# Token tiles 4 to 7 loaded a second time with channels on the partitions, normed in PSUM, their token rows rebuilt later on GpSimd

## The chip, the cores and the metric

The kernel runs on one core of a Trainium2 chip. The core has a matrix engine (PE), a vector engine (DVE), a scalar engine (ACT), GpSimd (POOL) and a queue engine (SP) from which nearly all DMAs are issued. The metric is the device time of one execution in microseconds, the median of several; lower is better. The kernel before takes 662.84 us (three runs, 662.69 to 662.87).

## The reference

One encoder layer on 1024 tokens of 1024 channels, in float32:

```
h    = layer_norm(x, emb_ln_g, emb_ln_b)             # the embedding norm
proj = h @ w_in     # q, k, v, z_attn, u, z_lru (512 columns each), g_attn, g_lru (1024 each)
attn = neighbourhood_attention(q, k, v, rpb)          # window 8 x 16 on a 16 x 64 grid, 8 heads
u    = centred_depthwise_conv(u, conv_w, conv_b)
hid  = rg_lru(u, forward) + rg_lru(u, reverse)        # decay rate: C * softplus(-lru_lambda)
m    = sigmoid(g_attn + b0) * ((attn * silu(z_attn)) @ w_ba)
     + sigmoid(g_lru + b1) * ((hid * silu(z_lru)) @ w_bb)
out  = layer_norm(alpha * h + m @ w_out, ln_g, ln_b)
```

The change touches the first line, the order of the first projections behind it, and the small polynomial for softplus(-lru_lambda).

## The kernel before, in words

**Numbers.** Every float32 operand of PE is split in two parts of PE's reduced float32 type, `_h` (a cast) and `_l` (the rest, a subtraction), and a product is three matmuls: high by high, low by high, high by low (`mm3`, L133). So each operand costs one cast (ACT or POOL) and one subtraction (DVE or POOL) before PE can use it.

**Tokens.** Eight tiles of 128 tokens. Tile i arrives token-major (`load_x`: 128 tokens on the partitions, 1024 channels along the row, 512 KB). The norm's mean and variance come from DVE (`ln_stats`, L223 to L225), the root from ACT (L229), 1/root refined on DVE (L237 to L239). Tiles 0, 1 and 3 are scaled on DVE with the gains in PSUM (L244, L247). Tiles 2 and 4 to 7 are scaled on ACT (L254) and get gain and offset on POOL (L260, four passes of 128x512). The finished tile is stored to DRAM (`keep`, `h_d`) for the residual at the end of the kernel; the store frees one of five buffers (tag `x`) for a later `load_x`. Then PE turns the tile in eight 128x128 transposes (`turn`, L271) into two PSUM banks, `tp{i}_0` and `tp{i}_1`, channels on the partitions; ACT casts these to `B..[0]` (`turn_hi`, L280), DVE makes `B..[1]` (`turn_lo`, L127).

**First products.** With the turned tiles PE computes v for each tile in 24 matmuls (`v_part`: kinds `h`, `w`, `a`, 8 each, L327; `a` uses the low parts) and a first part of q (`q_part`, four quarters of 24 matmuls of 512 columns each; the first quarter is done in two halves of 256 columns). The first two quarters need tiles 0 to 3, the last two need 4 to 7.

**Strassen's sums.** The other projections run as 17 pairs, each with seven products of 12 matmuls (`product`; one product is one *slot* of the schedule). They need sums of the turned tokens, T1, T2, T3 (from `t_full`, tiles 4 to 7, L300 to L304) and T4 (`t_last`, L308, L309), each split into high and low (`t_hi` on ACT, L313; `t_lo` on POOL). In pair 0 slot 0 and 1 use B11 and B21; T2, T1, T3 come in slots 2 to 4 and T4 in slot 6. The weights of pair p+1 are summed (`s_sum`, L385, DVE), cast (`s_hi`, L390) and split (`s_lo`) while pair p runs; a low part is made five slots ahead of its product.

**What sets the order.** All five engines run in the order in which the program text issues (`manual_schedule`), with semaphores between them. There is no planner; an instruction that waits holds back all behind it on its engine, SP's DMA issues too. From slot 0 on, work is hung into slots by hand (`at(slot, pos, f)`). PSUM has eight banks: `ps0` (0 to 3) for v and q, the others for `tp`; from slot 0 six banks go round for the products.

**Start.** PE begins with 18, 4 and 6 small bf16 matmuls on zeros (`warm_up`, L203, `WARM`), between them transposes that spread the norm's gains (`gps`, L212).

Of the kernel before, what the change touches and what calls it, by code (L numbers as in the profile page):

```python
# [45 lines left out]

SM_CW, SM_CB, SM_GB, SM_LAM, SM_BM, SM_N = 0, 16, 20, 36, 44, 60
HALVES = ((slice(0, 64), slice(64, P)), (slice(64, P), slice(0, 64)))
# [18 lines left out]
@with_exitstack  # L67
def encoder_kernel(ctx, tc, x, gb1, gb, w_qk, w_v, w_s, w_ba, w_bb, w_gate, smalls, bias, w_out, out):
    nc = tc.nc
# [42 lines left out]
    V.memset(eps_z, EPS * TWICE * TWICE)  # L112
    A.activation(warm, eps_t, AF.Sqrt)
    sm = cst.tile([P, SM_N], F32, name="sm")

# [10 lines left out]
    def lo_of(eng, lo, full, hi):  # L126
        eng.tensor_tensor(lo, full, hi.bitcast(F32), ALU.subtract)  # L127
# [103 lines left out]
    def ln_sums(i):  # L231
        ln_stats(i)
        ln_root(i)
# [28 lines left out]
    def keep(i):  # L262
        SP.dma_start(h_d[i], xs[i][:])

    tps = {}

# [23 lines left out]
    def f(t, i):  # L290
        return t[:, :, ti(i)].bitcast(F32)

    def t_full(i):

        tag = ("a22", "a21", "a12", "a22")[i - 4]
        tt[i, 3] = wsp.tile([P, 4, P], F32, tag=tag, bufs=2 if tag == "a22" else 1, name=f"t3_{i}")[:]
# [3 lines left out]
        A.copy(t3, tp4(i, 0))  # L300
        V.tensor_tensor(t1, tp4(i, 0), f(B11[0], i), ALU.subtract)
        V.tensor_tensor(t1, t1, f(B11[1], i), ALU.subtract)
        V.tensor_tensor(t2, tp4(i, 1), t1, ALU.subtract)
        V.tensor_tensor(t3, tp4(i, 1), t3, ALU.subtract)  # L304

    def t_last(i):
        t4 = tt[i, 4] = tt[i, 2]
        V.tensor_tensor(t4, f(B21[0], i), t4, ALU.subtract)  # L308
        V.tensor_tensor(t4, t4, f(B21[1], i), ALU.add)  # L309
# [58 lines left out]
    def s_load(p, *names):  # L368
        for z, o in enumerate(names if p < N_PAIR else ()):
            if p:  # L370
                t = wsp.tile([P, 4, P], F32, tag=o, bufs=2 if o == "a22" else 1, name=f"{o}_{p}f")[:]
            else:
                if z == 0:
                    place = dict(pool=ln, tag="x", bufs=5) if o == "a21" else dict(pool=wpl, tag="ws", bufs=1)
                    both = place.pop("pool").tile([P, 2, 4, P], F32, name=f"{o}_{p}f", **place)
# [11 lines left out]
    def s_hi(p, o):  # L387
        if p < N_PAIR:
            s_w[p, o] = pair(wsp, [P, 4, P], f"w{o}_{p}", tag="w" + o)
            (G.tensor_copy if p and o in HI_POOL else A.copy)(s_w[p, o][0][:], s_a[p, o])  # L390

    def s_lo(p, o):
        if p < N_PAIR:
            hi, lo = s_w[p, o]
            lo_of(G if p and o in LO_POOL else V, lo[:], s_a[p, o], hi[:])

# [109 lines left out]

    def tile_in(i):
        for kk in BOTH:
            turned_in(i, kk)

    def tile_lo(i):
        for kk in BOTH:
            turn_lo(i, kk)

    def ln_next(i):
        ln_sums(i)
        ln_scale(i)
# [37 lines left out]
    v_store(3)
    keep(6)
    q_part(0, 0, slice(256, HALF))
    tile_in(5)
    q_hi(0, 0)
    t_hi(4, 2, 1, 3)  # L560
    t_lo(4, 2, 1, 3)
    tile_lo(5)
    q_lo(0, 0)
    q_store(0, 0)
    keep(7)
    t_full(5)
    q_part(1, 0)
    q_hi(1, 0)
    q_lo(1, 0)
    q_store(1, 0)  # L570
    t_hi(5, 2, 1, 3)
    t_lo(5, 2, 1, 3)
    for kind in "hwa":
        v_part(4, kind, KS)
    tile_in(6)
    v_hi(4)
    tile_lo(6)
    v_lo(4)
    v_store(4)
    t_full(6)  # L580
    t_hi(6, 2, 1, 3)
    t_lo(6, 2, 1, 3)
    for kind in "hwa":
        v_part(5, kind, KS)
    s_load(0, "a11", "a12")
    tile_in(7)
    v_hi(5)
    tile_lo(7)
    v_lo(5)
    v_store(5)  # L590
    t_full(7)
    t_hi(7, 2, 1, 3)
    t_lo(7, 2, 1, 3)
    s_load(0, "a21", "a22")
    s_load(1, "a21")
    for kind in "hwa":
        v_part(6, kind, KS)
    v_hi(6)
    v_lo(6)
    v_store(6)  # L600
    s_load(1, "a12")
    s_sum(0, "s1", "s2", "s3", "s4")
    for kind in "hwa":
        v_part(7, kind, KS)
    v_hi(7)
    v_lo(7)
    v_store(7)
    s_load(1, "a11")
    for o in OPS[:3]:
        s_hi(0, o)  # L610
        s_lo(0, o)
    q_part(0, 1)
    for o in OPS[3:5]:
        s_hi(0, o)
        s_lo(0, o)
    q_hi(0, 1)
    q_lo(0, 1)
    q_store(0, 1)
    s_load(1, "a22")
    q_part(1, 1)  # L620
    for o in OPS[5:]:
        s_hi(0, o)
        s_lo(0, o)
    t_last(4)
    q_hi(1, 1)
    t_hi(4, 4)
    t_last(5)
    q_lo(1, 1)
    q_store(1, 1)
    for i in (5, 6, 7):  # L630
        if i > 5:
            t_last(i)
        t_hi(i, 4)
    for i in (7, 4, 5, 6):
        t_lo(i, 4)
    for pl in (ln, wpl, hb12, pst, ps0):
# [6 lines left out]
    lru = pool("lru", "right")  # L643
    sp = lru.tile([P, 8], F32, name="sp")
    nsp = lru.tile([P, 8], F32, name="nsp")
    t0, t1, t2 = (lru.tile([P, 8], F32, name=f"sp{c}") for c in range(3))
    lam = sm[:, SM_LAM:SM_LAM + 8]

    def decay_rates():
        V.tensor_scalar(smh[:], sm[:, SM_BM:SM_BM + 16], 0.5, None, ALU.mult)  # L650
        V.tensor_scalar(t0[:], lam, -1.0, None, ALU.mult)
        V.tensor_tensor(t0[:], lam, t0[:], ALU.min)
        A.activation(t0[:], t0[:], AF.Exp)
        yield
        V.tensor_scalar(t1[:], t0[:], 2.0, None, ALU.add)
        V.reciprocal(t1[:], t1[:])
        V.tensor_tensor(t0[:], t0[:], t1[:], ALU.mult)
        V.tensor_tensor(t1[:], t0[:], t0[:], ALU.mult)
        V.tensor_scalar(t2[:], t1[:], 1.0 / 21.0, 1.0 / 19.0, ALU.mult, ALU.add)
        yield  # L660
        for n in (17, 15, 13, 11, 9, 7, 5, 3, 1):
            V.tensor_tensor(t2[:], t2[:], t1[:], ALU.mult)
            V.tensor_scalar(t2[:], t2[:], 1.0 / n, None, ALU.add)
            if n in (13, 7, 1):
                yield
        V.tensor_tensor(t2[:], t2[:], t0[:], ALU.mult)
        V.tensor_scalar(t0[:], lam, -1.0, 0.0, ALU.mult, ALU.max)
        V.scalar_tensor_tensor(t0[:], t2[:], 2.0, t0[:], ALU.mult, ALU.add)
        V.tensor_scalar(sp[:], t0[:], C_LRU, None, ALU.mult)
        V.tensor_scalar(nsp[:], t0[:], -C_LRU, None, ALU.mult)  # L670
        yield
# [122 lines left out]
    def gate_stage(t, d, slot):  # L794
# [38 lines left out]
        def tables():  # L833
            A.activation(warm[:], eps_t[:], AF.Sigmoid)

# [111 lines left out]
    def gates_b(j):  # L947
# [3 lines left out]
             lambda: take_u(2), gates_b(0), lambda: take_zg(zb_d, 2, "zb"), gates_a(2), gates_b(1),  # L951
             lambda: take_k(0), gates_a(3), lambda: take_k(2), lambda: take_zg(za_d, 2, "za"), gates_b(2), gates_b(3)]
    rates = decay_rates()
    for slot in range(8, 14):
        at(slot, 1, lambda: next(rates))
# [807 lines left out]
```

## Time and profile before

| | |
|---|---|
| runs | 662.84 us median (662.69 to 662.87) |
| profiled execution, its own time | 663.5 us |
| its span, first to last instruction | 661.7 us |
| granted TensorE clock | 0.996 |
| busy: PE, DVE, ACT, POOL | 649.5, 521.6, 389.0, 396.7 us |
| slot 0 of pair 0 (first `a` matmul, timeline) | 82.78 us |

A timeline row gives the start, the duration, engine and line, the operation with output and inputs, a count, and in brackets the idle time before it with what ended it. Matmul durations overlap, since PE pipelines: the distance between two starts is what a matmul costs. The span is 1.8 us shorter than the execution's own time, and that execution was 0.66 us longer than the median.

### The profile page before, as it was taken

To read this page: it belongs to the slowest core of one execution; us is meant where nothing else is said; L and a number is where in the kernel's file an instruction comes from. 1 tells how busy PE (TensorE), PEld (TensorE's weight loads), DVE (VectorE), ACT (ScalarE), POOL (GpSimd) and SP (SyncE) were. 2 spreads that over 40 slices of the span, in tenths; PEclk is the share of its full clock that TensorE was granted. 3 is DMA by queue.
4 is the path that set the end of the run, shared out by engine and by line. 5 is a ranking of instruction groups with operands and counts; after the bars stand their busy time and mean duration, and the time that the engine had idled before them with its cause. 6 is when DMAs were issued, how large, how long until landed. Compare 5 with 4: busy or idle time off the path is not lost.

```text
span 661.7 us, 9464 instructions
## 1 busy us (share of the span) xinstructions
PE 649.5 (98%) x3119; PEld 543.5 (82%) x3119; DVE 521.6 (79%) x860; ACT 389.0 (59%) x686; POOL 396.7 (60%) x311
## 2 busy tenths in 40 slices
PE   8999999999999999999999999999999999999994
PEld 7888888888888887888788888888898888888883
DVE  7978867786899599879987696277877876994776
ACT  5564433356786677777666834277777744573242
POOL 6799263434676476658556455013552549989857
PEclk9999999999999999999999999999999999999998
DMA  8747607033334133532361548898977298333023
GB/s 324 271 140 250 195 33 257 15 111 128 125 113 135 57 112 99 188 111 81 132 220 59 192 163 281 306 342 272 362 264 240 68 306 294 113 113 127 24 104 128
DMA packets 52482, 113.42 MB, mean 171 GB/s; under 512 B 5505, under 2 KB 9937, under 8 KB 50897
## 3 DMA queue, kind: packets, MB, share of 16 engines
q1 hardware_dynamic: 51968, 112.28, 49.0%
q8 instruction: 25, 0.41, 0.2%
q10 hardware_dynamic: 464, 0.53, 0.2%
q14 instruction: 25, 0.20, 0.1%
HBM read 77.11 MB, written 35.68 MB: 170 GB/s over the span
## 4 chain that ended last, share of the span: by engine, by line
PE 86%; DVE 7%; POOL 2%; issue 1%; ACT 1%; DMA 1%; POOLq 0%; DVEq 0%; ACTq 0%
PE a L133 32%; PE s L133 12%; PE mb L133 12%; PE x L133 6%; PE w L133 5%; PE v L327 4%; PE s L1107 3%; PE acc L1155 3%; PE pt L1129 3%; PE q L133 2%; PE g L805 2%; POOL x L260 1%; DVE ws_l L127 1%; DVE uc L763 1%; PE tp L271 1%
## 5 line engine op out<-in xcount | busy, mean ns | idle before, releaser
L133 PE MATMUL a<-ht_h,ws_h 128*128 128x512 f32 x136 | 53.1, 391 | 0.0
L133 PE MATMUL a<-ht_l,ws_h 128*128 128x512 f32 x136 | 52.9, 389 | 0.0
L133 PE MATMUL a<-ht_h,ws_l 128*128 128x512 f32 x136 | 52.9, 389 | 0.0
L133 PE MATMUL a<-b_l,wa_h 128*128 128x512 f32 x136 | 52.9, 389 | 0.0
L133 PE MATMUL a<-b_h,wa_h 128*128 128x512 f32 x136 | 52.9, 389 | 0.0
L133 PE MATMUL a<-b_h,wa_l 128*128 128x512 f32 x136 | 52.9, 389 | 0.0
L1117 DVE CUSTOM_DVE_ANT_0 sc<-s,bias 128x384 f32<-128x384 f32 (+1 forms) x64 | 33.5, 523 | 20.3 <-PE s L1107 11.4
L1136 ACT CAST pt_h<-pt 128x384 fp32r<-128x384 f32 x64 | 29.0, 453 | 23.8 <-PE pt L1129 19.3
L1122 ACT ACTIVATE p<-sc,summ 128x384 f32<-128x384 f32 (+1 forms) x64 | 37.9, 592 | 5.4 <-DVE summ L1117 5.0
L133 PE MATMUL mb<-ya,wb_h 128*128 128x512 f32 x128 | 39.7, 390 | 0.1
L913 POOL CAST wb_h<-wb 128x512 fp32r<-128x512 f32 x9 | 7.0, 781 | 47.2 <-DMA wb<-in_w_bb_dram 47.2
L127 DVE TENSOR_TENSOR pt_l<-pt,pt_h 128x384 fp32r<-128x384 f32 x64 | 33.3, 520 | 1.9 <-ACT pt_h L1136 1.6
L127 POOL TENSOR_TENSOR ht_l<-t,ht_h 128x512 fp32r<-128x512 f32 x16 | 21.9, 1406 | 18.2 <-ACT ht_h L313 18.2
L1521 POOL TENSOR_TENSOR z<-z,gb 128x512 f32<-128x512 f32 (+2 forms) x23 | 27.7, 1218 | 8.5 <-ACT z L1516 7.5
L327 PE MATMUL v<-wv,b_h 128*128 128x512 f32 x128 | 32.4, 395 | 0.4 <-ACT b_h L426 0.4
L1107 PE MATMUL s<-ks,qs 128*128 128x384 f32 (+1 forms) x128 | 31.7, 329 | 0.0
L133 PEld LDWEIGHTS a<-ht_h,ws_h 128*128 128x128 f32 x136 | 25.5, 188 | 5.9 <-issue 0.5
L1129 PEld LDWEIGHTS pt<-ident,p 128*128 128x128 f32 x176 | 23.1, 140 | 8.3
L133 PEld LDWEIGHTS a<-ht_l,ws_h 128*128 128x128 f32 x136 | 25.5, 188 | 5.3
L133 PEld LDWEIGHTS a<-b_h,wa_l 128*128 128x128 f32 x136 | 25.5, 188 | 5.3
L133 PEld LDWEIGHTS a<-b_h,wa_h 128*128 128x128 f32 x136 | 25.5, 188 | 5.3
L133 PEld LDWEIGHTS a<-b_l,wa_h 128*128 128x128 f32 x136 | 25.5, 188 | 5.3
(542 smaller groups left out, 2258.9 us busy)
## 6 DMA issues: line engine op xcount, KB each, us to landing
ks<-k_d SPq DMA_DIRECT2D x8, 1024.0 KB, 7.6
h_d<-x SPq DMA_DIRECT2D x8, 512.0 KB, 2.9
v_d<-vs SPq DMA_DIRECT2D x8, 512.0 KB, 3.2
q_d<-q SPq DMA_DIRECT2D x8, 512.0 KB, 3.2
ga_d<-ga SPq DMA_DIRECT2D x16, 256.0 KB, 2.1
gb_d<-gb SPq DMA_DIRECT2D x16, 256.0 KB, 2.4
k_d<-k SPq DMA_DIRECT2D x8, 512.0 KB, 5.1
qs<-q_d SPq DMA_DIRECT2D x8, 512.0 KB, 5.2
```

What stands on the lines that cost most here:

```text
L127: eng.tensor_tensor(lo, full, hi.bitcast(F32), ALU.subtract)
L133: PE.matmul(o, a, b, start=first and i == 0, stop=last and i == len(prods) - 1, skip_group_check=not (first and last))
L327: PE.matmul(vos[i][:], a, wv[kind == "w"][k][:], start=vn[i] == 0, stop=vn[i] == 23)
L805: PE.matmul(o[:, n, :], w[:, 2 * d + b, :], us[b][:, n * HALF:(n + 1) * HALF], start=z == 0, stop=z == 1)
L913: G.tensor_copy(hi[:], st[:])
L1107: PE.matmul(o[:, :P * len(near(t))], q[:, t * P:(t + 1) * P], k[:, z, keys], start=z == 0, stop=z == 1)
L1117: V.tensor_tensor_reduce(s[:, :w], o[:, :w], heads[h][2][:, b0:b0 + w], -1.0, 3.0e38, ALU.add, ALU.min, accum_out=sums[h][0][:, t:t + 1])
L1122: A.activation(probs[h % 2][t][:], scs.pop((h, t))[:, :w], AF.Exp, bias=sums[h][0][:, t:t + 1], scale=-1.0, accum_out=sums[h][1][:, t:t + 1])
L1129: PE.transpose(tp[:, n * P:(n + 1) * P], probs[h % 2][t][:, z * P:(z + 1) * P], ident[:])
L1136: A.copy(pt[0][:, span(b)], tps[h, b][:, :P * len(near(b))])
L1155: PE.matmul(acc[n][:, lo - n * HALF:hi - n * HALF], vvs[h // 2][:, b, h % 2, :], pt[:, a:a + hi - lo], start=b in (1, 6) and z == 0, stop= ...
L1521: G.tensor_tensor(z, z, gbs[c, n][:, part], (ALU.mult, ALU.add)[c])
```

## The change

Tiles 4 to 7 are loaded twice: token-major as before, now only for mean and variance, and channel-major (`xt`, a copy that the host lays out, 128 channels on the partitions, `[P, 8, 128]`, 512 KB). PE no longer turns them. It spreads the 128 means and the 128 values of 1/root over the partitions (`spread`, two transposes of a broadcast column into one bank `bcp`). DVE subtracts the mean (`centred`, two passes of 128x512, one operand in PSUM), POOL multiplies by 1/root (two passes), and ACT applies gain and offset, which are now one number per partition, in eight passes of 128x128 that write the banks `tp{i}_0` and `tp{i}_1` (`affine`). Casting and splitting go on as before. The gains stand in `smalls` (16 more columns).

The token-major rows that the residual needs are made later: in slots 1 to 15 the four tiles are loaded a third time, scaled on ACT with the kept mean and 1/root, get gain and offset on POOL (16 passes), and are stored to `h_d`.

Other parts: the six matmuls of the third `warm_up` are left out; v of tiles 2 and 3 is cut in pieces between the spreads, and v of tiles 4 and 5 come together; `t_hi` of tiles 4 and 5 goes from ACT to POOL; T4 (`t_last`) is formed in PSUM (`pst4`, four banks), and its low parts go from POOL to DVE, with one cast of it; two of pair 0's low weights go from DVE to POOL; the casts of pairs 1 and 2 go from POOL to ACT; the softplus polynomial goes from DVE in slots 8 to 13 to POOL in slots 12 to 20.

```
-WARM = 18, 4, 6
+WARM = 18, 4, 0
+TOKENS_AT = ((1, 3, (4, 4, 5, 5)), (2, 5, (6, 6, 7, 7)), (3, 7, (8, 8, 9, 9)), (9, 11, (12, 12, 13, 13)))
+RATES_AT = (12, 13, 14, 15, 16, 17, 20)
+FIRST_POOL = ("a22", "s4")
+FIRST_ACT = (1, 2)
...
+    def sts_rest(i):
+        ln_rstd(i)
+        st, mv, sd, ve = sts[i]
+        V.tensor_scalar(kept[:, 2 * i - 8:2 * i - 7], mv[:, 0:1], -1.0, sd, ALU.mult, ALU.mult)
+        V.tensor_copy(kept[:, 2 * i - 7:2 * i - 6], sd)
+
+    def spread(i):
+
+        bcp[i] = pst.tile([P, HALF], F32, tag="bank", name=f"bcp{i}")
+        for z, col in enumerate((sts[i][1][:, 0:1], sts[i][2])):
+            PE.transpose(bcp[i][:, z * P:(z + 1) * P], col.to_broadcast([P, P]), ident[:])
+
+    def spread_copy(i):
+        bcs[i] = wsp.tile([P, 1, P], F32, tag=f"s{i - 3}", name=f"bc{i}")
+        A.copy(bcs[i][:, 0], bcp[i][:, P:2 * P])
+
+    def centred(i):
+
+        for kk in range(2):
+            t = xts[i][:, 4 * kk:4 * kk + 4, :]
+            V.tensor_tensor(t, t, bcp[i][:, :P].unsqueeze(1).to_broadcast([P, 4, P]), ALU.subtract)
+            G.tensor_tensor(t, t, bcs[i][:].to_broadcast([P, 4, P]), ALU.mult)
+
+    def affine(i, *kks):
+        for kk in kks or BOTH:
+            tps[i, kk] = pst.tile([P, HALF], F32, tag="bank", name=f"tp{i}_{kk}")
+            for k4 in range(4):
+                k = 4 * kk + k4
+                g, b = (sm[:, SM_LN + 8 * z + k:SM_LN + 8 * z + k + 1] for z in range(2))
+                A.activation(tps[i, kk][:, k4 * P:(k4 + 1) * P], xts[i][:, k, :], AF.Identity, bias=b, scale=g)
+            turn_hi(i, kk)
...
     def t_hi(i, *cs):
         for c in cs:
-            A.copy(Ts[c][0][:, :, ti(i)], tt[i, c])
+            (V.tensor_copy if (i, c) == (7, 4) else G.tensor_copy if i < 6 and c < 4 else A.copy)(Ts[c][0][:, :, ti(i)], tt[i, c])
...
     def t_lo(i, *cs):
         for c in cs:
-            lo_of(G, Ts[c][1][:, :, ti(i)], tt[i, c], Ts[c][0][:, :, ti(i)])
+            lo_of(G if c < 4 else V, Ts[c][1][:, :, ti(i)], tt[i, c], Ts[c][0][:, :, ti(i)])
...
     load_x(4)
     SP.dma_start(sm[:], smalls)
+    load_xt(4)
...
-    ln_next(5)
-    for kind in "hwa":
-        v_part(2, kind, KS)
-    keep(4)
-    ln_next(6)
...
+    v_part(2, "h", KS)
+    v_part(2, "w", KS)
+    spread(4)
+    spread_copy(4)
+    centred(4)
+    qk_prep(1)
+    stats_t(5)
+    v_part(2, "a", KS)
+    v_part(3, "h", KS)
+    v_part(3, "w", K0)
+    spread(5)
+    spread_copy(5)
+    stats_t(6)
+    centred(5)
+    v_hi(2)
+    v_part(3, "w", K1)
+    v_part(3, "a", K0)
+    spread(6)
...
+    def tokens_scaled(i):
+        n = 2 * i - 8
+        A.activation(hw[i][:], hw[i][:], AF.Identity, bias=kept[:, n:n + 1], scale=kept[:, n + 1:n + 2])
+
+    def tokens_gained(i, z, c):
+        t = hw[i][:, halves[c]]
+        G.tensor_tensor(t, t, ln_row[z][:, halves[c]], (ALU.mult, ALU.add)[z])
...
-    for slot in range(8, 14):
+    for slot in RATES_AT:
         at(slot, 1, lambda: next(rates))
```

Three places where the order on an engine differs. The first is PE at the end of the high parts of v of one tile; `x_175` is tile 4's token buffer, `v_559` is v of tile 3 before, `v_488` v of tile 2 in the change. Before:

```order
L327 MATMUL v_559<-wv_140,b_h 128x512
L327 MATMUL v_559<-wv_141,b_h 128x512
L271 MATMUL tp_0_579<-ident,x_175 128x128 x4
L271 MATMUL tp_1_585<-ident,x_175 128x128 x4
L327 MATMUL v_559<-wv_126,b_l 128x512
```

In the change (line numbers are those of the new text):

```order
L384 MATMUL v_488<-wv_146,b_h 128x512
L384 MATMUL v_488<-wv_147,b_h 128x512
L294 MATMUL bcp_505<-ident,ln4m 128x128
L294 MATMUL bcp_505<-ident,ln4e 128x128
L384 MATMUL v_488<-wv_132,b_l 128x512
```

Eight transposes of the tile have become two of its statistics, one tile of v earlier; the same holds for tiles 5, 6 and 7. The second place is DVE between the low part of v of tile 1 and the end of tile 6's statistics. Before:

```order
L127 TENSOR_TENSOR vs_426<-v_328,vs_426 128x8x64
L223 BN_STATS ln5t<-x_256 128x6 x2
L224 BN_AGGR ln5m<-ln5t 128x2
L225 TENSOR_SCALAR ln5e<-ln5m 128x1
L237 RECIPROCAL ln5e<-ln5e 128x1
L238 TENSOR_SCALAR ln5e<-ln5e 128x1
L239 TENSOR_SCALAR ln5e<-ln5e 128x1
L253 TENSOR_SCALAR ln5e<-ln5m,ln5e 128x1
L223 BN_STATS ln6t<-x_313 128x6 x2
```

In the change:

```order
L133 TENSOR_TENSOR vs_428<-v_330,vs_428 128x8x64
L304 TENSOR_TENSOR xt_184<-xt_184,bcp_505 128x512 x2
L229 BN_STATS ln5t<-x_258 128x6 x2
L230 BN_AGGR ln5m<-ln5t 128x2
L231 TENSOR_SCALAR ln5e<-ln5m 128x1
L243 RECIPROCAL ln5e<-ln5e 128x1
L244 TENSOR_SCALAR ln5e<-ln5e 128x1
L245 TENSOR_SCALAR ln5e<-ln5e 128x1
L287 TENSOR_SCALAR kept<-ln5m,ln5e 128x1
L288 COPY kept<-ln5e 128x1
L229 BN_STATS ln6t<-x_315 128x6 x2
```

Tile 4's two subtractions stand ahead of tile 5's statistics, and each tile has one small copy more. The third place is ACT behind the casts of the early tiles, in the change; `xt_184` is tile 4's channel-major copy:

```order
L298 COPY bc_508<-bcp_505 128x128
L176 CAST wqk_h<-wqk_s 128x1024
L235 ACTIVATE ln5e<-ln5m,few 128x1
L298 COPY bc_555<-bcp_552 128x128
L235 ACTIVATE ln6e<-ln6m,few 128x1
L391 CAST vs_574<-v_488 128x8x64
L298 COPY bc_587<-bcp_584 128x128
L313 ACTIVATE tp_0_589<-xt_184,sm 128x128 x4
L339 CAST b_h<-tp_0_589 128x4x128
```

Where one pass of 128x1024 (L254) and two casts stood for a tile, there are now a copy, eight passes of 128x128 and the two casts, and tile 4's first pass stands behind tile 6's spread.

More of the change, by code (lines that the diff above doesn't have):

```diff
@@ L113, in encoder_kernel @@
     A.activation(warm, eps_t, AF.Sqrt)
+    kept = cst.tile([P, 8], F32, name="kept")
+    sp, nsp, t0, t1, t2 = (cst.tile([P, 8], F32, name=f"sp{c}") for c in range(5))
     sm = cst.tile([P, SM_N], F32, name="sm")
@@ L600, in encoder_kernel @@
     v_store(6)
+    t_hi(7, 2, 1, 3)
+    t_lo(7, 2, 1, 3)
     s_load(1, "a12")
@@ L612, in encoder_kernel @@
     q_part(0, 1)
-    for o in OPS[3:5]:
+    for o in ("s1", "s3", "a22", "s4"):
         s_hi(0, o)
         s_lo(0, o)
+    t_places(4)
+    T1, T2, T3, T4 = (Ts[c] for c in (1, 2, 3, 4))
+    pst.release()
+    pst = tc.alloc_tile_pool(name="pst4", bufs=1, space=bass.MemoryType.PSUM, reuse_waits="tile")
+    for i in (7, 6, 5, 4):
+        tt[i, 4] = pst.tile([P, HALF], F32, name=f"t4_{i}")[:].rearrange("p (k t) -> p k t", k=4)
     q_hi(0, 1)
```

205 lines of the change are left out of this document (117 added, 88 removed).

## The prediction

> **What bounds the kernel now.** I read the page first: busy shares, then the chain that ended last.
>
> ```profile
> PE 649.5 (98%) x3119; PEld 543.5 (82%) x3119; DVE 521.6 (79%) x860; ACT 389.0 (59%) x686; POOL 396.7 (60%) x311
> PE 86%; DVE 7%; POOL 2%; issue 1%; ACT 1%; DMA 1%; POOLq 0%; DVEq 0%; ACTq 0%
> ```
>
> PE is busy for 98% of the span. A share is a mean, so next the busy times by stretch:
>
> ```profile
> 0.00:15.00 15.00, 13.04 (x79) 11.40 (x80) 10.90 (x27) 7.75 (x17) 8.45 (x13) 1.00 0.86 317
> ...
> 83.00:285.00 202.00, 202.00 (x888) 165.86 (x887) 169.06 (x216) 123.26 (x159) 113.67 (x86) 1.00 0.34 114
> 285.00:330.00 45.00, 44.64 (x196) 36.36 (x195) 41.33 (x37) 33.21 (x43) 31.56 (x19) 1.00 0.32 112
> 425.00:540.00 115.00, 114.77 (x690) 100.73 (x689) 87.80 (x238) 79.06 (x220) 44.18 (x41) 1.00 0.77 268
> 540.00:661.70 121.70, 112.43 (x508) 93.40 (x506) 90.03 (x162) 56.16 (x116) 103.72 (x82) 0.98 0.39 136
> ```
>
> The columns are the stretch, its length, and PE, its weight loads, DVE, ACT, POOL, then granted clock, DMA share and GB/s. PE loses 2.0 us in the first 15, 0.4 and 0.2 from 285 on, and 9.3 at the end, where the last norm runs. From 83 us on the change touches nothing that PE does, and PE has no gap worth winning there. So the time follows the moment at which slot 0 starts (82.78 us before), as long as DVE, ACT, POOL and the loads keep up behind it. The sum is therefore PE's own sequence up to slot 0, and its waits.
>
> **The change part by part.** *Start.* Six small matmuls go.
>
> ```profile
> 7.42 0.62 PE L203 MATMUL clock<-zero 128*128 128x128 bf16 x6
> 7.88 0.61 PE L271 MATMUL tp<-ident,x 128*128 128x128 f32 x4
> 9.20 0.69 DVE L127 TENSOR_TENSOR b_l<-tp,b_h 128x512 fp32r<-128x512 f32 x1 [0.28 <-ACT b_h L426]
> 14.33 0.63 PE L271 MATMUL tp<-ident,x 128*128 128x128 f32 x4 [0.30 <-DVE x L247]
> ```
>
> They cost PE 0.46 us from start to start. Behind them the path runs over ACT's cast to DVE, which waited 0.28 us for it, and DVE then runs without a gap to the norm for which PE waits at 14.33. DVE can come forward only by those 0.28, so I take 0.28 (bounds 0 and 0.46).
>
> *Transposes taken away.* Tiles 4 to 7 are turned in four groups of eight; one of them is split by a wait.
>
> ```profile
> 35.84 1.03 PE L271 MATMUL tp<-ident,x 128*128 128x128 f32 x8
> 36.63 2.07 PE L327 MATMUL v<-wv,b_l 128*128 128x512 f32 x8
> 41.42 0.60 PE L271 MATMUL tp<-ident,x 128*128 128x128 f32 x4
> 42.38 0.66 PE L271 MATMUL tp<-ident,x 128*128 128x128 f32 x4 [0.37 <-POOL x L260]
> 42.80 0.47 PE L133 MATMUL q<-b_h,wqk_h 128*128 128x512 f32 x1
> ...
> 60.14 1.03 PE L271 MATMUL tp<-ident,x 128*128 128x128 f32 x8
> 60.93 0.48 PE L327 MATMUL v<-wv,b_h 128*128 128x512 f32 x1
> ```
>
> The first and the last group here cost 0.79 us, as does one between them; the one at 41.42 costs 1.38 with its wait for POOL: 3.75 us.
>
> *Transposes added.* Four spreads of two, at 0.79 / 8 = 0.10 us each: 0.8 us. A broadcast column as the weights stood in the trace only at the start, at half the speed:
>
> ```profile
> L212 PEld LDWEIGHTS gps<-ident,gb_col x16: 226/226/226, 3.9 to 7.0; 128*128 128x128 f32 x16
> L271 PEld LDWEIGHTS tp<-ident,x x64: 137/140/143, 7.8 to 60.8; 128*128 128x128 f32 x64
> ```
>
> If that were the price of the broadcast, eight would cost 1.7 us. All 64 others ran at 140 ns, so I hold it for the slow clock of the first microseconds and take 0.8 (bounds 0.8 and 1.7). PE's own sequence is thus 0.28 + 3.75 - 0.8 = 3.2 us shorter.
>
> *New waits.* A spread needs the tile's 1/root from DVE. With everything 0.28 us earlier PE reaches the 16 transposes of tiles 2 and 3 at 24.72 and the sixteen matmuls behind them at 26.38 (these rows before, and DVE's in the same stretch):
>
> ```profile
> 25.00 1.91 PE L271 MATMUL tp<-ident,x 128*128 128x128 f32 x16
> 26.66 3.90 PE L327 MATMUL v<-wv,b_h 128*128 128x512 f32 x16
> 30.40 1.98 PE L327 MATMUL v<-wv,b_l 128*128 128x512 f32 x8
> 32.21 3.79 PE L327 MATMUL v<-wv,b_h 128*128 128x512 f32 x16
> 30.40 0.68 DVE L127 TENSOR_TENSOR vs<-v,vs 128x512 fp32r<-128x512 f32 x1
> 31.00 1.27 DVE L223 BATCH_NORM_STATS2 ln5t<-x 128x6 f32<-128x512 f32 x2
> 33.38 0.21 DVE L239 TENSOR_SCALAR ln5e<-ln5e 128x1 f32<-128x1 f32 x1
> 33.76 0.68 DVE L223 BATCH_NORM_STATS2 ln6t<-x 128x6 f32<-128x512 f32 x1
> L303 DVE TENSOR_TENSOR t<-tp,t 128x512 f32<-128x512 f32 x4 | 2.8, 692 | 0.1
> L302 DVE TENSOR_TENSOR t<-t,b_l 128x512 f32<-128x512 f32 x4 | 4.8, 1197 | 0.1
> ```
>
> Sixteen matmuls take 3.74 us, eight 1.81, one 0.227. PE: spread 4 at 30.1, spread 5 at 30.4 + 20 x 0.227 = 34.9, spread 6 at 35.2 + 1.8 = 37.0. DVE: its 31.00 becomes 30.8 (0.28 earlier, one small copy of about 0.1 later). Two subtractions come first; they are nearest to L303, which also has one operand in PSUM and starts its successor 0.6 us later; L302, with both in SBUF and POOL busy, is the other bound (1.2). So tile 5's statistics start at 32.0, and its 1/root stands 33.59 - 31.00 = 2.6 us later: 34.6, in time for 34.9. Tile 6's start 2.9 us after tile 5's (2.76 before, plus the copy), 34.9, and its 1/root is there at 37.5, with the semaphore 37.6. Spread 6 therefore waits about 0.4 us (one of its two transposes needs the mean alone). With L302's price for the subtractions both spreads are late by 1.2 more; with tile 6's x late it grows one for one. I take 0.4 (bounds 0 and 1.6). Spread 7 comes some 9 us later, behind q, and its bank is free once DVE has read `tp4_0`, which I put a good microsecond ahead of it.
>
> *What lies beside other work.* ACT gets eight passes of 128x128 for a tile in place of one of 1.25 us:
>
> ```profile
> L1516 ACT ACTIVATE w<-z,ve,sd x4: 442/762/765, 620.9 to 654.9; 128x512 f32<-128x512 f32 x3, 128x128 f32<-128x128 f32 x1
> L254 ACT ACTIVATE x<-x,ln5e 128x1024 f32<-128x1024 f32 x1 | 1.2, 1247 | 1.0 <-DVE ln5e L253 1.0
> 45.00:83.00 38.00, 38.00 (x177) 31.64 (x176) 31.75 (x45) 18.99 (x37) 24.23 (x18) 1.00 0.57 194
> ```
>
> The 128x128 form that writes PSUM took 0.44 us. Each waits for the one before it, so some 0.47 x 8 = 3.8 us a tile, 10 us more for four tiles against 1.25 x 4; ACT had 19 us free in the 38 of the last row. From spread 6 at 37.9 on, tile 4 is cast by 44, tile 5 by 50, tile 6 by 56, tile 7 by 62, and PE asks for them at about 47, 53, 58 and 64: the cover is 2 to 3 us, and a tile that is later than that is a wait of PE. On DVE, T4's low parts (four of 0.6 us and a cast) come on top of its last stretch before the slots, but slot 1 needs only tile 4's part of T4 read out of its bank, slot 3 tile 5's, slot 6 the rest. POOL's 16 token passes and 26 small ones in slots 4 to 20 stand before low weights that are due five slots of 2.7 us later. The extra loads (2 MB of `xt`, 2 MB of x, 1 MB of gains) fall into stretches with the DMA share at 0.3 to 0.6, except the first 512 KB, which stand ahead of a store that frees tile 5's buffer:
>
> ```profile
> SPq L188 <- DMA h_d<-x: 12.8, 2, 8.6
> 24.30 0.33 SPq L188 DMA_DIRECT2D x<-in_x_dram  x1
> x<-in_x_dram SPq DMA_DIRECT2D x6, 512.0 KB, 4.3
> ```
>
> SP waits up to 8.6 us for such a store, and tile 6's load comes behind tile 5's. At the 317 GB/s of the first stretch 512 KB are 1.6 us, so tile 6's load goes from 24.30 to 25.9 and lands 4.3 us later, at 30.2; it is read at 34.9. All these I set to 0.
>
> *Sum.* 3.2 - 0.4 = 2.8 us; I take 2.7, since a wait I have not seen is likelier than one less. The profiled execution's 663.5 becomes 660.8 (span 659.0), and the median, 0.66 below that execution, **660.2 us**.
>
> **The rivals.** *One: the new feed is late.* DVE and ACT are the bound in place of PE: subtractions at L302's price make spreads 5 and 6 wait 1.6 us in all, and a tile that ACT finishes 1 us after PE asks for it takes the rest: 3.2 - 2.6 = 0.6 us gained, 662.2. For it speaks that DVE must deliver within tenths; against it that L303's form never took more than 0.7 with POOL busy.
>
> *Two: slower, DVE starved by POOL in slots 4 to 13.* DVE's operations with two SBUF inputs get long when POOL works:
>
> ```profile
> L127 DVE TENSOR_TENSOR wa_l<-a_11f,wa_h 128x512 fp32r<-128x512 f32 x1 | 2.9, 2885 | 0.0
> L127 DVE TENSOR_TENSOR ws_l<-s_11f,ws_h 128x512 fp32r<-128x512 f32 x4 | 5.9, 1478 | 0.0
> L662 DVE TENSOR_TENSOR sp<-sp,sp 128x8 f32<-128x8 f32 x8 | 1.3, 165 | 0.2
> 93.90:118.60 24.70, 24.70 (x109) 20.12 (x109) 20.11 (x51) 6.82 (x12) 10.50 (x12) 1.00 0.53 182
> ```
>
> About 13 such operations fall into those ten slots (27 us). At 2.9 us each in place of 0.7 they add 29 us to DVE's roughly 17 (20.11 of 24.70, less some 26 small operations of the polynomial at 0.17, scaled to 27), 19 more than the slots last. Low weights have five slots, 13.6 us, of cover, so PE would wait 5.4 us: 660.2 + 5.4 = 665.6, slower. It decides from about 2.7 us for each (where the excess reaches 13.6 us plus the 2.7 gained). Against it: in the trace 2.9 is the extreme, 1.5 a high mean. [...]
>
> *Three: the clock comes late.* If the six matmuls are what raises the clock, PE runs at half speed for one more stretch like that of the sixteen L212 (3.4 us): 1.7 us lost, 0.3 of it in the wait at 14.33: 661.6. Against it, the weight loads were slow up to 7.0 and fast from 7.8, with only transposes in the 3.4 us before. [...]
>
> *Four: the change doesn't do what it says*, the token passes being late for the end: the rows are read after 570 us and stored near 125, so I give it nothing.
>
> **How the numbers follow.** Forecast 0.66, its own range 659.2 (nothing waits, and the later 0.6 us of PE's gaps shrink too) to 661.2; rival one 0.17, two 0.09, three 0.06, the rest unknown. The range goes to 662.2, with rival one inside. A measurement of this kernel tells 0.2%, 1.3 us, from no change: faster means below 661.5. That holds for nearly all of the forecast (0.65), half of rival three, and a part of rival one and of the unknown (0.08): 0.76. Slower, above 664.2: most of rival two and a little of the unknown, 0.09. Same: 0.15.
>
> **What would show it.** Slot 0's first `a` matmul at about 80.0 us; the spreads' weight loads near 140 ns; a wait of PE for DVE of some 0.4 us at spread 6 and none at v of tiles 4 to 7; the first `tp` at about 7.6; no new PE gaps from 85 to 540 us. A slot 0 at 80 with the old end would mean rival two; slot 0 near 82, rival one. The prediction is wrong if PE waits over 1.5 us in all for DVE or ACT between 25 and 83 us.

## The result

The changed kernel takes 667.83 us (six executions, 666.71 to 668.37) against 662.86 for the kernel before: a ratio of 1.0071, 95% interval 1.0061 to 1.0082. It is 5.0 us slower, where 2.7 us less were forecast.

The gain forecast up to slot 0 is there, and the loss lies behind it. From the page after and its stretches (columns as in the prediction):

```profile
PE 648.8 (97%) x3089; PEld 540.8 (81%) x3089; DVE 534.1 (80%) x851; ACT 405.4 (61%) x725; POOL 415.6 (62%) x337
83.00:285.00 202.00, 198.22 (x859) 162.28 (x858) 170.16 (x191) 130.03 (x169) 133.86 (x110) 0.98 0.41 140
```

Between 83 and 285 us, where PE had no idle time before (202.00 of 202.00), it now loses 3.8 us, and the granted clock is 0.98. POOL has 20 us more to do there than the 113.67 before. PE's timeline after shows the place: the spread's wait and the start of slot 0, then the end of slot 19 and the start of slot 20.

```profile
37.59 0.32 PE L294 MATMUL bcp<-ident,ln6e 128*128 128x128 f32 x1 [0.38 <-DVE ln6e L245]
...
80.20 0.50 PE L139 MATMUL a<-b_h,wa_h 128*128 128x512 f32 x1 [0.16 <-DVE q L416]
...
134.94 0.39 PE L139 MATMUL s<-b_l,ws_h 128*128 128x512 f32 x1
139.01 0.80 PE L139 MATMUL a<-ht_h,wa_h 128*128 128x512 f32 x1 [3.68 <-DVE c L767]
...
144.73 0.44 PE L139 MATMUL a<-b_h,wa_l 128*128 128x512 f32 x1
```

Slot 0 starts at 80.20 us, 2.58 earlier than before. Slot 20 starts 4.07 us after the last matmul of slot 19, 3.84 more than a matmul costs. The thirteen steps from 139.01 to 144.73 take 5.72 us in place of 13 x 0.227 = 2.95: PE runs at half speed, 2.77 us more. The stretches around it give the clock in the column behind the five engines:

```profile
135.00:139.00 4.00, 0.33 (x2) 0.00 (x0) 2.38 (x4) 1.05 (x2) 3.74 (x8) 0.87 0.00 0
139.00:144.00 5.00, 4.99 (x12) 3.94 (x13) 4.40 (x7) 1.63 (x2) 2.52 (x4) 0.50 0.79 262
```

The clock's records have one stretch of 6.83 us at 0.5 there, from 137.98 to 144.81 us, and no such stretch inside the kernel before: 1.00 from 7.66 to 656.19 us, 0.50 behind that. By the trace, then, 2.77 us are paid on top of the idle time; a run below tests it.

Why was DVE's pass `c` (L767, it empties the bank) late? DVE's timeline:

```profile
126.26 1.28 DVE L834 SCALAR_TENSOR_TENSOR uc<-up,sm,uc 128x1024 f32<-128x1024 f32 x1
131.90 1.77 DVE L133 TENSOR_TENSOR wa_l<-a_3f,wa_h 128x512 fp32r<-128x512 f32 x1 [4.36 <-POOL wa_h L448]
...
137.06 0.69 DVE L133 TENSOR_TENSOR ws_l<-s_3f,ws_h 128x512 fp32r<-128x512 f32 x1 [1.58 <-POOL ws_h L448]
137.68 0.68 DVE L776 SCALAR_TENSOR_TENSOR zb<-zb,a 128x512 f32<-128x512 f32 x1
138.27 0.69 DVE L767 TENSOR_TENSOR c<-u,a 128x512 f32<-128x512 f32 x1
```

DVE stands 4.36 and 1.58 us in front of two splits of pair 3's weights, each waiting for a cast on POOL, and `c` stands behind them in DVE's order. POOL's timeline after, first and last rows, and the same cast before (last row, of the kernel before):

```profile
94.03 12.04 POOL L1042 TENSOR_TENSOR hw<-hw,ln_row 128x512 f32<-128x512 f32 x8 [6.19 <-ACT ws_h L448]
...
112.93 9.13 POOL L1042 TENSOR_TENSOR hw<-hw,ln_row 128x512 f32<-128x512 f32 x6
122.02 0.65 POOL L727 TENSOR_TENSOR sp<-sp,sp 128x8 f32<-128x8 f32 x1
...
131.26 0.61 POOL L448 CAST wa_h<-a_3f 128x512 fp32r<-128x512 f32 x1
...
136.42 0.61 POOL L448 CAST ws_h<-s_3f 128x512 fp32r<-128x512 f32 x1
```

```profile
126.93 0.61 POOL L390 CAST wa_h<-a_3f 128x512 fp32r<-128x512 f32 x1 [3.04 <-issue]
```

POOL works without a gap from 94.03 us on; sixteen token passes stand ahead of the polynomial, and both ahead of pair 3's cast. Before, POOL was idle for 3 us ahead of that cast and did it at 126.93, when PE was 2.6 us later.

One more loss comes at the entrance to the attention. DVE's last pass over the bank of slot 117, and the last projections of the output on the chain, before and after:

```profile
417.77 0.70 DVE L696 TENSOR_TENSOR c<-u,a 128x512 f32<-128x512 f32 x1 [5.20 <-PE a L133]
638.68 10.89 PE x L133 x48
```

```profile
422.07 0.70 DVE L767 TENSOR_TENSOR c<-u,a 128x512 f32<-128x512 f32 x1 [5.20 <-PE a L139]
643.58 10.89 PE x L139 x48
```

The kernel is 4.30 us behind at the first of these and 4.90 at the second. So: -2.58 (slot 0) + 3.84 (PE's wait) + 2.77 (half clock) + 0.27 (a remainder in the slots that no single wait accounts for) + 0.60 (behind 422 us) = 4.90 us.

### The profile page after: what moved, and what is told of

Read it like the earlier page. It is cut to its first block, busy times and chain, and to the rows that moved or that the text cites. A ratio compares the mean times of both kernels' runs of the same rounds, so it can differ in the third digit from the quotient of the medians.

```text
span 666.4 us, 9482 instructions
## 1 busy us (share of the span) xinstructions
PE 648.8 (97%) x3089; PEld 540.8 (81%) x3089; DVE 534.1 (80%) x851; ACT 405.4 (61%) x725; POOL 415.6 (62%) x337
## 4 chain that ended last, share of the span: by engine, by line
PE 75%; DVE 11%; POOL 6%; issue 3%; ACT 3%; DMA 2%; POOLq 0%; SPq 0%; DVEq 0%; ACTq 0%
PE a L139 28%; PE mb L139 12%; PE s L139 10%; PE x L139 6%; PE w L139 5%; PE acc L1256 3%; POOL hw L1042 3%; PE s L1208 3%; PE pt L1230 3%; PE g L876 2%; PE v L384 2%; DVE ws_l L133 1%; ACT tp L313 1%; DMA g<-gb_d 1%; DVE wa_l L133 1%
## 5 line engine op out<-in xcount | busy, mean ns | idle before, releaser
L139 PE MATMUL a<-ht_h,wa_h 128*128 128x512 f32 x68 | 28.0, 412 | 4.0 <-DVE c L767 3.7
```

What stands on the lines that cost most here:

```text
L139: PE.matmul(o, a, b, start=first and i == 0, stop=last and i == len(prods) - 1, skip_group_check=not (first and last))
```

## The experiments

Three theories of the wait at 135 us. **A, POOL's queue:** pair 3's casts are late because they stand behind the token passes and the polynomial. **B, slow neighbours:** DVE is late because its own operations get long beside a busy POOL (`wa_l` above 1.77 us, `c` 0.69). **C, the loads:** pair 3's weights come late behind the token stores in SP's queue. The ratios are against the kernel before on the same chip.

**Pair 3's casts on ACT.**

```
-FIRST_ACT = (1, 2)
+FIRST_ACT = (1, 2, 3)
```

> Only edit: the five high casts of pair 3's weights go from POOL to ACT, like those of pairs 1 and 2; the 16 token passes, the polynomial and everything else stay. Theory A (POOL's queue order): in the changed kernel POOL worked without a gap from 94.0 to 137.2 us, and pair 3's first cast stood in that queue behind the token passes and the polynomial (131.26 us), so DVE waited 4.4 and 1.6 us for two casts, emptied PE's bank late, PE waited 3.7 us and then ran 6.8 us at half clock. ACT was idle for 3.8 us before 127.27 and 5.0 us before 135.5, so the casts are early there: PE's wait of 3.7 us and the half clock go, 667.8 - 3.7 - 3.4 = 660.7 us (660.0 to 661.5). Theory B (DVE is slow because POOL is busy beside it: its operations with two SBUF inputs take 1.1 to 1.8 us in place of 0.69): POOL is as busy as before, the bank stays late and PE still waits 2 us or more, time above 664. Theory C (pair 3's weights arrive late behind the token stores in SP's queue): no change, 667.8.

661.79 us, ratio 0.998 (0.997 to 0.9989). DVE's timeline of this kernel, and POOL's row with the same work as before:

```profile
127.76 0.68 DVE L133 TENSOR_TENSOR wa_l<-a_3f,wa_h 128x512 fp32r<-128x512 f32 x1
...
130.18 1.78 DVE L133 TENSOR_TENSOR ws_l<-s_3f,ws_h 128x512 fp32r<-128x512 f32 x1
...
133.02 0.69 DVE L767 TENSOR_TENSOR c<-u,a 128x512 f32<-128x512 f32 x1 [0.47 <-PE a L139]
```

```profile
136.42 1.26 POOL L732 TENSOR_TENSOR sp<-sp,sp 128x8 f32<-128x8 f32 x1
```

POOL is as late as before with its polynomial, DVE's splits take up to 1.78 us, and still `c` now waits for PE and not PE for `c`. So A, and B as it was put falls: DVE's long operations alone cost PE nothing here. The wait and the half clock are gone, 6.0 us. But 1.1 us of the gain expected for this run are missing; that is for the runs on the entrance, below.

**The polynomial back on DVE.**

```
-RATES_AT = (12, 13, 14, 15, 16, 17, 20)
+RATES_AT = (8, 9, 10, 11, 12, 13, 14)
...
-            G.tensor_tensor(t2[:], t2[:], t1[:], ALU.mult)
-            G.tensor_scalar(t2[:], t2[:], 1.0 / n, None, ALU.add)
+            V.tensor_tensor(t2[:], t2[:], t1[:], ALU.mult)
+            V.tensor_scalar(t2[:], t2[:], 1.0 / n, None, ALU.add)
```

> Only edit: the softplus polynomial and the two small operations behind it go back to DVE, in slots 8 to 14, as they stood before the change; POOL keeps the 16 token passes and pair 3's casts. Theory A: POOL is through the token passes near 122 us and reaches pair 3's first cast near 125 us in place of 131; DVE gets some 28 operations of 0.17 to 0.2 us (5 us) in a stretch where it was full (12.8 of 13.0 us from 106 to 119) but has 4.4 us free in the next 13; no wait of PE over 1 us, 660.7 us (660.0 to 662.5). Theory B: DVE has more to do beside a busy POOL, PE's wait is as long or longer, 667.8 or more. Theory C: 667.8.

670.19 us (666.47 to 672.23), ratio 1.0112 (1.0086 to 1.0138): a miss for A. Rows of PE, DVE and POOL of this kernel:

```profile
119.22 0.50 PE L139 MATMUL a<-ht_h,wa_h 128*128 128x512 f32 x1 [2.90 <-DVE up L758]
```

```profile
113.43 1.15 DVE L729 TENSOR_SCALAR sp<-sp 128x8 f32<-128x8 f32 x1
...
117.39 0.16 DVE L732 TENSOR_TENSOR sp<-sp,sp 128x8 f32<-128x8 f32 x1
...
118.48 0.69 DVE L758 TENSOR_TENSOR up<-u,a 128x512 f32<-128x512 f32 x1
...
120.21 1.23 DVE L732 TENSOR_TENSOR sp<-sp,sp 128x8 f32<-128x8 f32 x1
```

```profile
118.45 5.57 POOL L1042 TENSOR_TENSOR hw<-hw,ln_row 128x512 f32<-128x512 f32 x4 [3.90 <-ACT hw L1038]
...
129.44 1.42 POOL L448 CAST wa_h<-a_3f 128x512 fp32r<-128x512 f32 x1 [2.64 <-PE a L139]
```

POOL does reach pair 3's cast with time to spare (it waits 2.64 us for PE there), as A has it. But another wait of the same kind takes its place seven slots earlier: DVE's queue was full, and the pass `up` that empties a bank stands behind small operations of which some take 1.2 us in place of 0.17. In the 3.9 us in which POOL idles ahead of 118.45 all of them are short; the long ones lie beside its passes. I had counted five microseconds and a slack that lies behind 119 us, too late for them. Here DVE is starved while POOL is dense, in the slots that the prediction's rival two named. The rows are of the fastest of the four executions (666.47 us), with a wait of 2.90 us and one stretch of 3.41 us at half clock; what the other three (668.96 to 672.23, granted clock 0.989 to 0.991) lost beyond that has no trace and stays open.

**The polynomial later on POOL.**

```
-RATES_AT = (12, 13, 14, 15, 16, 17, 20)
+RATES_AT = (12, 13, 18, 19, 20, 21, 23)
```

> Only edit: the polynomial stays on POOL, but its four last parts come in slots 18 to 23 in place of 14 to 20, most of it behind pair 3's casts. Theory A: pair 3's first cast is on POOL near 125 us, no wait of PE over 1 us there; the polynomial may now hold up pair 4's casts a little: 660.7 us (660.0 to 663). Theory B and C: as much work as before on the engines up to 137 us less some 20 small operations, so a wait of 2 us or more stays, above 664.

662.42 us, ratio 0.9988 (0.9979 to 0.9998). POOL's cast comes at

```profile
126.25 1.07 POOL L448 CAST wa_h<-a_3f 128x512 fp32r<-128x512 f32 x1
```

and PE waits 0.3 us for `c`. Five microseconds earlier on POOL are enough. The same work in another order costs 5.4 us less: A again.

**Without the token passes.**

```
-            at(slot, 1, lambda i=i, z=z, c=c: tokens_gained(i, z, c))
+            pass
```

> The 16 token passes on POOL are left out (gain and offset of the token rows of tiles 4 to 7 for the residual are missing), loads, ACT passes and stores of these rows stay, and the polynomial stays on POOL in slots 12 to 20. Theory A: without the passes (28 us from 94 to 122) POOL has no backlog, and the polynomial alone does not hold up pair 3's casts: no wait, 660.5 us (659.8 to 661.5). Theory B: 660.5 as well, since POOL is mostly idle. Theory C (SP's queue and the loads, which are unchanged): 667.8.

661.68 us, ratio 0.9976 (0.9966 to 0.9986). The loads and stores are all there and PE has no wait at slot 20, so C falls. POOL's cast comes at

```profile
127.78 0.61 POOL L448 CAST wa_h<-a_3f 128x512 fp32r<-128x512 f32 x1
```

The polynomial alone still takes POOL from 118.58 us to this cast, and DVE still waits 0.97 and 1.58 us for pair 3's casts; `c` ends at 135.49, just in time for slot 20 at 135.58. The time is only 0.1 us below that with the casts on ACT, a kernel that has all sixteen passes: once nothing urgent stands behind them, they cost nothing that can be told from the noise.

**Filling the wait.** Is the half clock a second price, or only a record?

```
+    def filler():
+        o = psd.tile([P, 2, HALF], F32, tag="gates", name="filler")
+        for n in range(15):
+            PE.matmul(o[:, n % 2, :], B11[0][:, 0, :P], B11[0][:, 0, :], start=True, stop=True)
+
+    at(20, 0, filler)
```

> The changed kernel with one addition: 15 matmuls of 128x512 on data that is already there, into two banks that nothing uses before slot 21, stand in PE's order ahead of slot 20's product, that is in the 3.7 us in which PE waits for the bank; their output is read by nobody. They take 15 x 0.227 = 3.4 us, all of it inside the wait. Theory A (the wait costs twice: 3.7 us of idleness and then 6.8 us at half clock, worth 3.4): PE has no idle window, the clock stays, and the time falls by 3.4 us though nothing of the wait is removed: 664.4 us (663.9 to 665.2). Rival (the low clock behind the wait is only a record and does not lengthen the run, or comes whether PE idles or not): 667.8 or more.

664.92 us, ratio 1.0027 (1.0019 to 1.0036). PE's timeline, and the stretch that had 0.50 in the changed kernel:

```profile
135.27 3.56 PE L1064 MATMUL filler<-b_h 128*128 128x512 f32 x15
138.97 0.50 PE L139 MATMUL a<-ht_h,wa_h 128*128 128x512 f32 x1
139.31 0.39 PE L139 MATMUL a<-ht_h,wa_l 128*128 128x512 f32 x1
```

```profile
139.00:144.00 5.00, 5.00 (x22) 4.15 (x23) 4.41 (x7) 2.72 (x4) 2.52 (x4) 1.00 0.78 259
```

Slot 20 starts at 138.97, as late as in the changed kernel (139.01), but at full clock, and the time is 2.9 us lower. The wait for the bank is untouched; what went is the second price, 2.77 by the trace. By the traces PE ends 3.49 us earlier (640.09 in place of 643.58 for the row of `x` above): 2.77, and the 0.6 us at the entrance to the attention, where PE does not wait in this kernel.

**A made wait.** How long may PE idle before that happens? On top of the casts on ACT:

```
+    def made_gap():
+        t = lru.tile([P, 2, HALF], F32R, tag="r", name="gap")
+        A.copy(t[:, 0, :], ub[2]["s1"][:])
+        A.copy(t[:, 1, :], t[:, 0, :].bitcast(F32))
+        o = psd.tile([P, 2, HALF], F32, tag="gates", name="gap_o")
+        PE.matmul(o[:, 0, :], t[:, 1, :P], t[:, 1, :], start=True, stop=True)
+
+    at(20, 0, made_gap)
```

> The kernel with pair 3's casts on ACT (no wait of PE over 0.8 us in the slots), and a wait made on purpose: behind slot 19's product ACT copies its bank twice in a row (2 x 0.6 us, behind DVE's own pass over that bank), and one matmul of PE that nobody reads waits for the second copy ahead of slot 20. PE should idle about 2.3 us there. Known so far: waits up to 1.05 us from start to start bring no low clock, one of 2.9 us brought one stretch of 3.41 us, one of 4.07 us two of them. If a wait of 2.3 us already brings a stretch of half clock: 661.8 + 2.3 + 1.7 = 665.8 us, with 3.4 us at 0.5 in the clock's records. If not: 664.1 us and no such record.

665.24 us, ratio 1.0032 (1.0021 to 1.0043), and the ten executions fall into two groups: five from 664.05 to 664.73 at a granted clock of 0.995 to 0.997, five from 665.75 to 666.48 at 0.992 to 0.994. The profiled one (664.29) belongs to the first and has no low clock:

```profile
137.56 0.51 PE L1066 MATMUL gap_o<-gap 128*128 128x512 f32 x1 [2.06 <-ACT gap L1064]
```

By the times both expectations were right, each for half of the executions. The groups lie some 1.8 us apart, near the 1.7 that one stretch of 3.41 us at half clock would cost; that the slower five had such a stretch is an estimate from their times and mean clocks, since none of them has a trace. The changed kernel looks alike one step up: 666.71 and 666.77 us at 0.994 and 0.995, four executions from 667.72 to 668.37 at 0.990. The two low stretches inside a kernel that the records have last 6.83 us (the changed kernel) and 3.41 us (the polynomial on DVE). The first begins at 137.98 us, 1.03 ahead of PE's restart at 139.01. In the kernel with the polynomial on DVE PE restarts at 119.22 us, its steps come down to 0.23 us, and steps of 0.43 begin only at 120.68. So the low stretch did not begin at one fixed distance from the end of the wait. Why the same wait brings one in some executions and not in others is not shown: the wait that took 2.06 us in the trace without a low clock was, by the times, followed by one in half of the executions.

**The entrance to the attention.** With the casts on ACT, slot 0 starts 2.28 us earlier than before and the bank of slot 117 is emptied 2.07 earlier, but PE ends only 1.17 earlier. PE waits 0.7 us for DVE's `m`, and `m` for a load of a gate. The load shares queue q1 with the second head's q, bias and k (322 GB/s from 419.28 to 432.3 us in the changed kernel):

```
-    at(HEAD_AT, 1, lambda: load_head(1))
+    at(HEAD_AT + 5, 1, lambda: load_head(1))
```

> The kernel with pair 3's casts on ACT, and one more edit: the loads of the second attention head (q, bias, k: about 2 MB) are issued five slots later, behind the two gate loads for which DVE and then PE wait at the entrance to the attention (a wait of PE of 0.66 us at 427 us that the kernel before does not have). Theory: the gain of 2.1 us that slots 0 to 118 keep is cut by these loads, which land 1.0 us later against their issue than before; with less in the queues ahead of them the gates are there, PE's wait goes, and the time is 0.7 to 0.9 us below that with the casts alone: 661.0 us. Rival (the gates' late landing has another cause, or the attention is bound by the second head's loads): 661.8 or more.

660.60 us, ratio 0.9961 (0.9948 to 0.9975). DVE's first `m`, with the casts alone and with this edit:

```profile
426.39 0.69 DVE L1131 SCALAR_TENSOR_TENSOR m<-g,mb 128x512 f32<-128x512 f32 x1 [7.35 <-DMA g<-gb_d]
```

```profile
423.41 0.69 DVE L1131 SCALAR_TENSOR_TENSOR m<-g,mb 128x512 f32<-128x512 f32 x1 [4.74 <-PE mb L139]
```

`m` now waits for PE's own product and PE for nothing there. The time is 1.2 us below that with the casts alone, more than the 0.7 to 0.9 expected; by the traces PE ends 1.62 earlier, of which 0.38 stood already at the bank of slot 117, ahead of this edit. The same edit on the kernel before:

> The kernel before with one edit: the loads of the second attention head are issued five slots later, behind the two gate loads, as in the two fastest kernels so far. In the kernel before PE has no wait at the entrance to the attention (DVE waits 6.24 us for the gate load there, and is done just in time). If the entrance took 0.7 to 0.9 us only from kernels in which the gate load lands late against its issue: no change, 662.9 us (662.4 to 663.3). If PE is held there in the kernel before too, in a way that its waits do not show: 662.0 us.

662.92 us, ratio 1.0001 (0.9991 to 1.0011): nothing to win there, as the trace said. In the kernel before the gate load lands in time. From the pass `c` to `m` it is 427.36 - 417.77 = 9.59 us in the kernel before, 10.59 in the changed kernel and 10.69 with the casts on ACT, but 10.03 with the polynomial on DVE and 9.51 with the filler, and in the last two PE does not wait there. The order of the loads is the same in all of them. Why they land up to 1.1 us later in some kernels is left open.

**All of it, and q's split earlier.** In some of the traces slot 0 waits 0.16 to 0.37 us for the split of q's third quarter, which stands on DVE behind three splits of weights that are due later:

```
     for o in ("s1", "s3", "a22", "s4"):
         s_hi(0, o)
         s_lo(0, o)
+        if o == "s1":
+            q_hi(0, 1)
+            q_lo(0, 1)
...
-    q_hi(0, 1)
-    q_lo(0, 1)
     q_store(0, 1)
```

> The kernel with pair 3's casts on ACT and the second head's loads five slots later, and one more edit: cast and split of the third quarter of q come three weights earlier on ACT and DVE, since slot 0's bank waits for that split (0.16 to 0.37 us in the traces). Theory: slot 0 starts 0.2 to 0.35 us earlier, 80.0 us or below; with the later loads 660.7 us (660.2 to 661.4). Rival (the split only moves the wait on to the next bank or to the weights of slot 4): as without this edit, 661.0 or above.

660.13 us (659.86 to 660.63), ratio 0.9954 (0.9942 to 0.9967): 2.8 us below the kernel before and 7.7 below the changed one.

```profile
80.08 0.39 PE L139 MATMUL a<-b_h,wa_h 128*128 128x512 f32 x1
635.57 10.89 PE x L139 x48
```

Slot 0 starts without a wait, 2.70 us earlier than before, and PE ends 3.11 earlier. In the trace with the later loads alone slot 0 did not wait either and started at 80.15, so what the earlier split is worth is not shown: 0.07 us in these two traces, 0.47 in the medians, with intervals that overlap.

**The six warm-up matmuls put back**, in that kernel:

```
-WARM = 18, 4, 0
+WARM = 18, 4, 6
```

> The fastest kernel so far (pair 3's casts on ACT, later loads of the second head, earlier split of q's third quarter) with the third block of six warm-up matmuls put back, which the change left out. The prediction's first term: their removal brings 0.28 us (bounds 0 and 0.46), by the norm on DVE that PE waits for at 14 us. By it: slot 0 0.28 us later, 660.1 + 0.3 = 660.4 us. Rival (in the changed kernel PE waits 0.8 to 1.6 us for DVE at its first transposes, so the six matmuls would lie inside that wait): 660.1 us, slot 0 unchanged. Rival three of the prediction (without them the clock comes up late): faster, 659.5 us or below.

660.59 us, ratio 0.9962 (0.9947 to 0.9976), slot 0 at 80.22. That is 0.46 us more in the medians and 0.14 in slot 0's start. The intervals of the two ratios overlap, and the traces do not show the six matmuls as the reason. PE's first transposes without them and with them:

```profile
7.72 0.66 PE L330 MATMUL tp<-ident,x 128*128 128x128 f32 x4 [1.55 <-DVE x L253]
```

```profile
6.81 0.50 PE L209 MATMUL clock<-zero 128*128 128x128 bf16 x6
7.44 0.66 PE L330 MATMUL tp<-ident,x 128*128 128x128 f32 x4
...
12.03 1.02 PE L384 MATMUL v<-wv,b_h 128*128 128x512 f32 x3 [0.45 <-ACT wv L202]
```

The six lie in a stretch in which PE otherwise waits for DVE's norm, as the first of the two rivals has it, and the first transposes come no later with them (DVE's norm came 0.28 us earlier in that execution); the 0.14 at slot 0 come behind a wait of 0.45 us for a cast of v's weights. So the size of the prediction's first term is not shown by this pair. The time is not lower with the six, and the clock does not need them. The sixteen transposes L212 (L218 in the change) ahead of their place, before and in the changed kernel:

```profile
4.01 3.62 PE L212 MATMUL gps<-ident,gb_col 128*128 128x128 f32 x16
```

```profile
4.01 2.33 PE L218 MATMUL gps<-ident,gb_col 128*128 128x128 f32 x16
```

In the changed kernel the clock comes up while they run (their weight loads fall from 226 ns to 137 at 4.86 us; before, all sixteen took 226, the last at 7.00), earlier than before and without the six. So rival three falls.

## Why the prediction was wrong

**Right: the time and the path up to slot 0.** Forecast: slot 0 at about 80.0; measured 80.20. The first `tp` stood at 7.52 us (forecast 7.6), the transposes that waited for DVE's norm at 14.33 now stood at 14.03 (0.28 earlier forecast), the spreads at 30.12, 34.88 and, behind a wait of 0.38, 37.59 (forecast 30.1, 34.9, and 0.4 of wait at the third). The costs taken from neighbouring rows held too, by the groups of the changed kernel:

```profile
L294 PEld LDWEIGHTS bcp<-ident,ln4m x1: 134/134/134, 29.9 to 29.9; 128*128 128x128 f32 x1
L304 DVE TENSOR_TENSOR xt<-xt,bcp x8: 678/681/687, 30.9 to 51.5; 128x512 f32<-128x512 f32 x8
L313 ACT ACTIVATE tp<-xt,sm x32: 461/463/487, 38.1 to 60.7; 128x128 f32<-128x128 f32 x32
```

A broadcast column loads in 134 ns (140 taken, 226 the bound), a subtraction took 0.68 us with POOL at work (as L303, not as L302), an affine pass 0.46 (0.47 taken). PE waited for nothing at v of tiles 4 to 7. Only 0.16 us of wait for q stood at slot 0's own bank, which I had not looked at. With the 0.38 that makes 0.54 us of PE's waits for DVE between 25 and 83 us, where the prediction called itself wrong above 1.5: its sign watched the stretch that held.

**Wrong: the step that set POOL's 16 token passes and 26 small operations (24 by the change's own text) to 0**, because they "stand before low weights that are due five slots of 2.7 us later". In place of 0 it measured 3.84 us of PE's wait and 2.77 behind it. Three things were wrong in it. First, pair 3's high casts, not only low parts, stand behind them in POOL's queue, and behind a high cast waits DVE's split, and behind that, in DVE's order, the pass that frees PE's bank: there the cover is not five slots. Secondly I never added up the queue. At the 1.29 us of POOL's 128x512 passes, sixteen of them and the three low parts among them and the polynomial are 24.5 us, from POOL's start at 94.0 to 118.5; the fifteen operations of the polynomial ahead of the cast, at 0.2 to 0.3 us, end at 122 to 123. How late the cast may be, the runs show: at 126.25 PE waited 0.3 us (the polynomial later), at 127.78 not at all (no token passes, so that DVE's operations were shorter). By this estimate three to five microseconds of slack are left at the best prices, not thirteen, and the cast would still have been in time. Thirdly, and this used it up, the prices next to a busy DVE were mostly not the best ones:

```profile
L1042 POOL TENSOR_TENSOR hw<-hw,ln_row x16: 1287/1619/1836, 94.0 to 120.8; 128x512 f32<-128x512 f32 x16
L732 POOL TENSOR_TENSOR sp<-sp,sp x9: 202/204/1117, 124.1 to 135.9; 128x8 f32<-128x8 f32 x9
```

Nine of the sixteen passes took 1.62 to 1.84 us, the others 1.29 to 1.30, and the small operations between 0.20 and 1.1; the cast came at 131.26, some 8 us later than at the best prices. So, by this estimate, operations that get long beside the other engine have a part in it after all, on POOL's side: they made the queue long, and its order made PE wait.

**Rival two** had the right sign, put the loss behind slot 0 and came near the size (665.6), but by luck: it had the stretch wrong (slots 4 to 13; PE waited ahead of slot 20) and the mechanism, DVE slowed until low weights run out. The runs show DVE waiting for POOL's order; slow splits alone (up to 1.78 us), with the casts on ACT, cost PE nothing. Something like it came only in the kernel with the polynomial on DVE, by small operations and not by splits. The chance of 0.09 for slower was too low all the same: the argument against it looked at single durations and not at the sum of what POOL had to do.

**Missing: the half clock.** I reckoned with PE's waits at their length. The trace of before had shown slow weight loads (226 ns) only up to 7.0 us and a clock of 0.50 only behind 656.19, so nothing in the sum stood for it; it turned a wait of 3.84 us into 6.6.

**Missing: the entrance to the attention**, 0.6 to 0.9 us. "No new PE gaps from 85 to 540" was said of PE's own share of 100%, not of what else stood on the edge. DVE's wait of 6.24 us for a gate load was in the trace and ended just in time. With pair 3's casts and these loads mended the time comes to 660.60 us, and with the earlier split of q to 660.13, where 660.2 was forecast; that the last lies so near is partly luck, since the earlier split was no part of the forecast.

## What to carry to other kernels

When work is moved to an engine that has time on average, add up its queue in order and at the prices it has beside the other engines' work, from the moment it starts to the first instruction behind it that another engine waits for, and follow that instruction through the other engine's order to a bank that the bound engine needs. Move urgent casts off the queue (or bulk work behind them) before moving the bulk in; the same work then cost nothing measurable here. Here PE's waits were not always priced at their length: with one of 2.90 us stood 3.41 us at half clock, with one of 3.68 us 6.83, which cost 2.77 us more. So a loss in one place may be worth filling with useless matmuls if it can't be removed: here that brought 2.9 us.

## What was not expected of the hardware

PE's idle time of about 2.06 us brought, by the times, a stretch of half clock in five of ten executions, by estimate worth about 1.7 us; with 3.68 us of idle time came 6.83 us at half clock, for which 2.77 us were paid. A POOL operation on 128x8 numbers took from 0.20 us to 1.26 in the changed kernel, and one on DVE from 0.15 to 1.26 in the kernel with the polynomial there, the long ones always where the other engine was at work on tiles of 512 columns or more (on DVE 0.15 to 0.17 while POOL idled). Not all beside such work were long: DVE's at 107.53 and 122.72 us in the kernel with the polynomial on DVE took 0.16 and 0.17, each right behind a long one. By these rows the time of a small operation can hang on its neighbour more than on its size.
